# Operand addresses in SBUF: dense products of a two-block network, contiguous and at fixed offsets

## The chip, the cores and the metric

The kernel runs on one core of a Trainium2 chip. The metric is the device time of one execution in microseconds (us). Before the change the median of three runs is 1893.16 us (1890.84 to 1898.01).

## The reference, cut to what matters

The input is 256 tokens of width 1024, in float32. Two networks follow each other, each of two layers.

```python
# first network, layer i
h = rmsnorm(x, norm_mix_g[i])
mix = ...(h) @ w_out                     # layer 0: RWKV7 and gated delta rule; layer 1: banded attention
x = x + mix
x = x + square(relu(rmsnorm(x) @ mlp_w1[i])) @ mlp_w2[i]          # 1024 -> 4096 -> 1024
x = x + rmsnorm(p[i] @ ple_w_proj[i]) * sigmoid(x @ ple_w_gate[i])
# in layer 0's mixer a low-rank path reads the normed rows and the rows shifted by one token
dh = token_shift(h) - h
xw = h + dh * mu_lora[0]                 # likewise xa, xg;  then xw @ w1, xa @ a1, xg @ g1
# second network, layer i, on x and, in its layer 0, a second stream of 256 context tokens
x = x + gate * mixer(modulate(x)) @ w_out
x = x + gate * conv_ffn(modulate(x))     # up to 2 x 2816, a convolution over 3 tokens, silu * v, down
```

Nearly all the arithmetic is in the dense products with the weights `w_m` (MLP), `w_up` and `w_dn` (conv_ffn), and the projections of the mixers.

## The kernel before, in words

Activations lie feature-major: 128 features on the partitions, 256 tokens along a partition, and eight such slices make 1024 features. A dense product is made in float32r with both operands split in a high and a low part: `mm3` (line 433) issues high times high, low activation times high weight, high activation times low weight, each a matmul that loads 128 columns of weights and moves 256 columns of activations. Where two streams go together ("joint", `wide == 2`), one matmul moves 512 columns. `chunk` (line 442) goes over the output columns in pieces: a piece is 4 slices of 128 inputs by 256 outputs, so 24 matmuls. `weight` (line 420) issues a DMA of 512 KB from SP's queue into `raw` (4 buffers), and `split_w` lets ScalarE copy `raw` to `hi` and VectorE form `lo = raw - hi` (3 buffers each). `dense_tm` (line 1296) makes products token-major for attention: there the weights `hi`, `lo` are the moving operand, in runs of 256 columns, and the activations are loaded as weights.

The order of instructions on each engine is that of a scheduler, from priorities that the program sets; it interleaves small matmuls of the mixers (scores, transposes, recurrences) and of the norms with dense ones.

Where the operands lie, in bytes of a partition, in the built program:

- `act`, the tile of `acts` and `joint` (lines 529 and 534): rows of `T + 2` = 258 values, so 1032 bytes. `acts0` begins at 52800, `acts1` at 78272 (64 and 448 modulo 512), and each next slice lies 8 bytes further modulo 512 than the slice ahead of it.
- `hi` at 25792, 29888, 33984 and `lo` at 38080, 42176, 46272: all 192 modulo 1024, 4096 bytes long.
- `hh` and `hlo`, the 32 slices of the MLP's hidden activations (lines 1212 and 1213): rows of 256 values without a gap, at 107136 and 139904. Both are 128 modulo 512, and so is every slice.
- `fh` and `fl` in conv_ffn, as inputs of its first up-product (class `Early`, line 1740; 258 columns are used, two of them for a shift vector) and as hidden activations (`evac_v`, line 1840): rows of 1032 bytes, at many different offsets.

In `layer0_mixer` (line 992) the high and low parts `hh`, `hl_` are written from column 2 on, after GpSimd has set columns 0 and 1 to zero, so that `H` reads columns 2 to 257 and `HS`, the rows shifted by one token, columns 1 to 256 of the same tile. `lora` (line 1058) makes two products, `pa` from `H` and `pb` from `HS`, scales them with the row factors `rb` and `rbs` (the same factors, shifted) and adds them.

Of the kernel before, what the change touches and what calls it, by code (L numbers as in the profile page):

```python
# [10 lines left out]
F32 = mybir.dt.float32  # L11
# [8 lines left out]
P = 128  # L20
D = 1024
T = 256
KT = 8
NEG = -1.0e30
EPS = 1e-6
# [247 lines left out]
class K:  # L273
    def __init__(self, nc, tc, A, es):
        self.nc, self.tc, self.A, self.es = nc, tc, A, es
        self.cp = self.pool("const", 1)
        self.wraw = self.pool("wraw", 4)
        self.whi = self.pool("whi", 3)
        self.wlo = self.pool("wlo", 3)
        self.psG = self.pool("psG", 1, PSUM)  # L280
        self.sms = [self.pool(f"small{i}", 2) for i in range(3)]
        self.ap = [self.pool("acts0", 1), None]
        self.modp = self.pool("modp", 1)
        self.pse = None
        self.slots = None
        self.runs, self.head = False, None
        self.later, self.slow = [], []
# [131 lines left out]

    def weight(self, name, c, piece, kt, ncol, off=0):  # L420
        n = kt * ncol
        raw = self.wraw.tile([P, 1024], F32, name="raw")
        self.nc.sync.dma_start(out=raw[:, :n], in_=self.A[name][c, piece][:, off * ncol:off * ncol + n])
        return self.split_w(raw, n, kt)

    def split_w(self, raw, n, kt):
        hi = self.whi.tile([P, 1024], F32R, name="hi")
        lo = self.wlo.tile([P, 1024], F32R, name="lo")
        self.act(hi[:, :n], raw[:, :n])
        self.tt(lo[:, :n], raw[:, :n], hi[:, :n].bitcast(F32), ALU.subtract)  # L430
        return (hi[:, :n].rearrange("p (k n) -> p k n", k=kt), lo[:, :n].rearrange("p (k n) -> p k n", k=kt))

# [96 lines left out]
    def acts(self, i):  # L529

        t = self.ap[i].tile([P, 2, KT, T + 2], F32R, name="act", tag="act")
        return t[:, 0], t[:, 1]

    def joint(self):

        return [self.ap[i].tile([P, KT, 2, T + 2], F32R, name="act", tag="act") for i in range(2)]

# [74 lines left out]
def hl(h, l):  # L612
    return lambda j: (h[:, j], l[:, j])
# [378 lines left out]
def layer0_mixer(k, x, bg, ple):  # L992
# [20 lines left out]
    hh, hl_ = k.acts(0)  # L1013
    for t in (hh, hl_):
        nc.gpsimd.memset(t[:, :, 0:2].bitcast(F32), 0.0)
    st = k.stat_begin(None, "n0")
# [4 lines left out]
    for c in range(4):  # L1021
        xc = x[:, 2 * c:2 * c + 2]
        for e in range(2):
            j = 2 * c + e
            k.act(hh[:, j, 2:], xc[:, e], AF.Copy, scale=k.vec("gmix0", j))
            k.stt(hl_[:, j, 2:], xc[:, e], k.vec("gmix0", j), hh[:, j, 2:].bitcast(F32), ALU.mult, ALU.subtract)
    H = lambda j: (hh[:, j, 2:], hl_[:, j, 2:])
    HS = lambda j: (hh[:, j, 1:T + 1], hl_[:, j, 1:T + 1])
    rbp = big.tile([P, T + 2], F32, name="rbp")
    nc.gpsimd.memset(rbp[:, 0:2], 0.0)  # L1030
    rb, rbs = rbp[:, 2:], rbp[:, 1:T + 1]
    rb2 = rb[:, None, :].to_broadcast([P, 2, T])

    def norm():
        for c in range(4):
            k.stat_add(st, x[:, 2 * c:2 * c + 2], f2)
            yield
        k.norm_rows(st, rbp[:, 2:], lambda: f1("nt"))

# [18 lines left out]
    def lora():  # L1058

        pa, pb = (k.psD.tile([P, 2, T], F32, name="psx") for _ in range(2))  # L1060
        for half in range(2):
# [7 lines left out]
            k.tt(raw, raw, wb, ALU.subtract)  # L1069
            for src, X, ps in ((raw, H, pa), (wb, HS, pb)):  # L1070
                wh, wl = k.split_w(src, 1024, 4)
                for m in range(2):
                    ms = slice(m * P, (m + 1) * P)
                    for j in range(4):
                        k.mm3(ps[:, m], (wh[:, j, ms], wl[:, j, ms]), X(4 * half + j), half == 0 and j == 0 and m == 0, half == 1 and j == 3 and m == 1)
        z = w2.tile([P, 2, T], F32, name="dsh")
        k.tt(z, pb, rbs[:, None, :].to_broadcast([P, 2, T]), ALU.mult)
        k.tt(lt, pa, rb2, ALU.mult)
        k.tt(lt, lt, z, ALU.add)
        k.act(lt[0:64, 0], lt[0:64, 0], AF.Tanh)  # L1080
# [126 lines left out]
def mlp(k, l, x, xg, st, nxt, aside, aside2=None):  # L1207
# [3 lines left out]
    w2 = k.pool("mlpw", 2, es=es)  # L1211
    hh = hp.tile([P, 32, T], F32R, name="hh")
    hlo = hp.tile([P, 32, T], F32R, name="hlo")
# [83 lines left out]
def dense_tm(k, name, c, xs, evac):  # L1297

    ps = [k.psD.tile([P, 2, 256], F32, name="psx") for _ in xs]
    for pi in range(2):  # L1300
        wh, wl = k.weight(name, c, pi, 4, 256)
        for s, x in enumerate(xs):
# [437 lines left out]
class Early:  # L1740


    def __init__(self, k, mod, o, pool, n, s=0):
        self.k, self.mod, self.o, self.s = k, mod, o, s
        self.t = []
        for c in range(4):
            if 2 * c % n == 0:
                t = [pool.tile([P, n, T + 2], F32R, name=n_) for n_ in ("fh", "fl")]
            self.t.append([a[:, 2 * c % n:2 * c % n + 2] for a in t])
# [41 lines left out]
def conv_ffn(k, l, hs, hj, xs, mod, st0, sts, hp, early, between=None, out=None):  # L1791
# [36 lines left out]
    def evac_v(c, s, ps):  # L1828
# [10 lines left out]
        if c not in hid:  # L1839
            hid[c] = [hp.tile([P, 2 * ns, T + 2], F32R, name=n).rearrange("p (m s) t -> p m s t", m=2)[..., :T] for n in ("fh", "fl")]  # L1840
        k.split_act(hid[c][0][:, :, s], hid[c][1][:, :, s], o)
# [392 lines left out]
def program(nc, tc, A, out):  # L2234
    with ExitStack() as es:
        k = K(nc, tc, A, es)
        load_consts(k)
        k.mods = [k.modp.tile([P, 48, 2], F32, name=f"mod{l}") for l in range(2)]
        x = k.pool("xres", 1).tile([P, KT, T], F32, name="x")
# [54 lines left out]
```

## Time and profile before

| | |
|---|---|
| median of 3 runs | 1893.16 us (1890.84 to 1898.01) |
| profiled execution: its own time | 1898.16 us |
| profiled execution: span from first to last instruction | 1896.2 us |
| mean granted clock of TensorE | 0.985 |
| TensorE matmul / weight load busy | 1831.4 us / 1660.7 us |
| VectorE / ScalarE / GpSimd busy | 1383.3 us / 911.2 us / 75.4 us |
| moved by DMA | 292.13 MB, mean 154 GB/s |

Matmuls are pipelined: the profile's record of one lasts longer than the distance to the next one's start, so busy time and mean duration don't give the cost of a matmul in a full stream. What gives it is the distance from start to start, here called the **pace**: a stretch in which TensorE does nothing but one kind of matmul, divided by the number of matmuls in it. The windows view counts every instruction that touches the stretch; since a record is over two paces long, about two of those counted started ahead of it.

The groups of instructions are listed by line of the helper (`k.mm` is line 374 for every matmul), so a group is told by its tiles: `psx<-act,hi` is a matmul into the PSUM tile `psx` with `act` moving or loaded and `hi` as the other operand; the shape names the moving columns.

### The profile page before, as it was taken

The numbers are of one execution on the slowest core, as the hardware profiler recorded it, in microseconds if no ns is written. First come the engines' busy times: TensorE is split into PE (matmuls) and PEld (weight loads), VectorE is DVE, ScalarE is ACT, GpSimd is POOL, SyncE is SP. The second block draws the span as 40 slices with busy tenths as digits, with TensorE's granted clock in tenths as the row PEclk, the third lists the DMA queues.
The fourth block names the chain that finished last, engine by engine and source line by source line (L and its number), as shares of the span: only waits on it lengthen the run. The fifth ranks groups of instructions, "written<-read, shape, count | busy, mean of one in ns | idle before, by whom it ended". The sixth has DMA issues, their size and how long they took to land.

```text
span 1896.2 us, 36237 instructions
## 1 busy us (share of the span) xinstructions
PE 1831.4 (97%) x14540; PEld 1660.7 (88%) x14540; DVE 1383.3 (73%) x2874; ACT 911.2 (48%) x1526; POOL 75.4 (4%) x175
## 2 busy tenths in 40 slices
PE   7999999999999999999999897999999999899999
PEld 6777889999998899999988776878888998789998
DVE  6757668765687876768767888689785578977674
ACT  5433545554566755454545454433123444465443
POOL 0000010000000000000001100000000001100000
PEclk9999999999999999999999997999999999999999
DMA  8742414555563455654221122356872353334553
GB/s 314 269 163 106 139 57 130 187 189 191 190 212 127 158 194 188 195 190 163 84 65 49 36 72 86 100 210 196 275 252 89 123 185 127 100 101 151 184 189 123
DMA packets 80944, 292.13 MB, mean 154 GB/s; under 512 B 9255, under 2 KB 11144, under 8 KB 77448
## 3 DMA queue, kind: packets, MB, share of 16 engines
q1 hardware_dynamic: 80776, 289.82, 45.7%
q8 instruction: 114, 1.87, 0.4%
q14 instruction: 54, 0.44, 0.1%
HBM read 288.73 MB, written 1.05 MB: 153 GB/s over the span
## 4 chain that ended last, share of the span: by engine, by line
PE 86%; DVE 9%; ACT 2%; issue 1%; POOL 1%; DMA 1%; SPq 0%; ACTq 0%; DVEq 0%
PE psx L374 81%; DVE lo L364 3%; PE psx L377 2%; PE psg L1474 1%; PE psg L374 1%; ACT hi L361 1%; POOL qb L364 1%; DVE qx L364 0%; DVE mt L371 0%; DMA adaraw<-in_w_ada 0%; ACT act L361 0%; DVE act L371 0%; DVE act L364 0%; PE psg L377 0%; DVE qms L1329 0%
## 5 line engine op out<-in xcount | busy, mean ns | idle before, releaser
L374 PE MATMUL psx<-act,hi 128*128 128x256 f32 (+1 forms) x3872 | 821.0, 307 | 24.4 <-ACT hi L361 11.0
L361 ACT ACTIVATE hi<-raw 128x1024 fp32r<-128x1024 f32 (+1 forms) x440 | 453.8, 1032 | 631.9 <-PE psx L374 483.2
L364 DVE TENSOR_TENSOR lo<-raw,hi 128x1024 fp32r<-128x1024 f32 (+1 forms) x440 | 524.4, 1194 | 283.1 <-ACT hi L361 273.3
L374 PEld LDWEIGHTS psx<-act,hi 128*128 128x128 f32 x3872 | 630.4, 191 | 77.4 <-issue 14.4
L374 PE MATMUL psx<-act,lo 128*128 128x256 f32 (+1 forms) x1936 | 591.8, 306 | 4.8 <-DVE lo L364 4.8
L374 PEld LDWEIGHTS psx<-act,lo 128*128 128x128 f32 x1936 | 369.7, 191 | 29.0 <-DVE lo L364 7.3
L374 PE MATMUL psx<-hi,act 128*128 128x256 f32 x1280 | 242.1, 290 | 2.4 <-ACT act L361 1.5
L374 PEld LDWEIGHTS psx<-hi,act 128*128 128x128 f32 x1280 | 199.1, 191 | 10.4 <-issue 6.8
L374 PE MATMUL psx<-lo,act 128*128 128x256 f32 x640 | 181.0, 284 | 1.0 <-DVE lo L364 1.0
L374 PE MATMUL psx<-fh,hi 128*128 128x256 f32 (+2 forms) x528 | 162.3, 308 | 4.9 <-DVE xc L371 4.9
L374 PE MATMUL psx<-fh,lo 128*128 128x256 f32 (+2 forms) x528 | 162.3, 308 | 1.3 <-DVE lo L364 1.3
L374 PE MATMUL psx<-fl,hi 128*128 128x256 f32 (+2 forms) x528 | 161.7, 306 | 0.0
L374 PE MATMUL psx<-hh,hi 128*128 128x256 f32 x512 | 142.4, 278 | 0.0
L374 PE MATMUL psx<-hlo,hi 128*128 128x256 f32 x512 | 142.2, 278 | 0.0
L374 PE MATMUL psx<-hh,lo 128*128 128x256 f32 x512 | 142.2, 278 | 0.0
L374 PEld LDWEIGHTS psx<-lo,act 128*128 128x128 f32 x640 | 121.7, 191 | 1.2 <-DVE lo L364 1.2
L374 PEld LDWEIGHTS psx<-fh,hi 128*128 128x128 f32 x528 | 101.3, 192 | 10.9 <-issue 6.0
L374 PEld LDWEIGHTS psx<-fh,lo 128*128 128x128 f32 x528 | 101.2, 192 | 8.0 <-DVE lo L364 2.1
L374 PEld LDWEIGHTS psx<-fl,hi 128*128 128x128 f32 x528 | 101.3, 192 | 4.5
L374 PEld LDWEIGHTS psx<-hlo,hi 128*128 128x128 f32 x512 | 96.9, 189 | 0.0
L374 PEld LDWEIGHTS psx<-hh,hi 128*128 128x128 f32 x512 | 96.1, 188 | 0.0
L374 PEld LDWEIGHTS psx<-hh,lo 128*128 128x128 f32 x512 | 96.1, 188 | 0.0
(498 smaller groups left out, 2279.4 us busy)
## 6 DMA issues: line engine op xcount, KB each, us to landing
raw<-in_w_m SPq DMA_DIRECT2D x128, 512.0 KB, 4.3
raw<-in_w_up SPq DMA_DIRECT2D x92, 512.0 KB, 3.3
adaraw<-in_w_ada SPq DMA_DIRECT2D x24, 1024.0 KB, 6.2
adaraw<-in_w_ada SPq DMA_DIRECT2D x48, 512.0 KB, 4.3
raw<-in_w_dn SPq DMA_DIRECT2D x48, 512.0 KB, 3.4
raw<-in_w_ein SPq DMA_DIRECT2D x28, 512.0 KB, 5.5
raw<-in_w_ie SPq DMA_DIRECT2D x28, 512.0 KB, 3.3
raw<-in_w_qkv SPq DMA_DIRECT2D x24, 512.0 KB, 3.3
```

The costliest lines, as they stand in the source:

```text
L361: self.nc.scalar.activation(out=out, in_=in_, func=func, **kw)
L364: (eng or self.nc.vector).tensor_tensor(out=out, in0=a, in1=b, op=op)
L374: self.pe(lambda: self.nc.tensor.matmul(out=out, lhsT=lhsT, rhs=rhs, start=start, stop=stop))
L377: self.pe(lambda: self.nc.tensor.transpose(out=out, in_=in_, identity=self.ident))
L1474: k.pe(lambda: nc.tensor.matmul(out=ps[q:q + 32], lhsT=sv[:, 4 * pi + j], rhs=raw[:, j], start=pi == 0, stop=pi == 1, tile_position=(0, q)))
```

## The change

Every operand of a dense product becomes a contiguous run at one offset. `acts` and `joint` lose the two columns (rows of 1024 bytes), and a joint operand of 512 columns is one run. The two `mod` tiles move ahead of `acts0` and get padding of 40 values each, so that `acts0` lies at 60032 and `acts1` at 84608, both 128 modulo 512. The weight tiles become 1280 values long, so at 25792, 30912, 36032 and 41152, 46272, 51392: again 192 modulo 1024. `dense_tm` uses them from value 96 on: its moving weights lie at 64 modulo 512, the activations that it loads at 128. `fh` and `fl` get lead-in padding that puts them at 128 modulo 512 (in `Early` the second row of a pair, still 258 values long, is 8 bytes further). `hh` gets 112 values of lead-in; `hh` and `hlo` stay at 128 modulo 512.

In `layer0_mixer` there is no shifted operand: `pb` is made from `H` too, scaled with `rb`, and added to `pa` with a shift by one column (255 of 256 columns). Two memsets of `act` and one of `rbp` on GpSimd are gone.

On TensorE, VectorE, ScalarE and SP's queue the same instructions stand in the same order as before (TensorE 9119 rows in both, VectorE 2365, ScalarE 1059, SP 210). What is different is their addresses, some shapes (two runs of 256 become one of 512, the last addition of `lora` 2 x 255 in place of 512), and waits: three waits of TensorE on DMAs of the context tiles, issued long before, come in where a pool now overlaps another. GpSimd has three memsets fewer.

```diff
-    def weight(self, name, c, piece, kt, ncol, off=0):
+    def weight(self, name, c, piece, kt, ncol, off=0, pad=0):
...
-    def split_w(self, raw, n, kt):
-        hi = self.whi.tile([P, 1024], F32R, name="hi")
-        lo = self.wlo.tile([P, 1024], F32R, name="lo")
-        self.act(hi[:, :n], raw[:, :n])
-        self.tt(lo[:, :n], raw[:, :n], hi[:, :n].bitcast(F32), ALU.subtract)
...
+        return self.split_w(raw, n, kt, pad)
+
+    def split_w(self, raw, n, kt, pad=0):
+
+        hi, lo = (p.tile([P, WLEN], F32R, name=nm)[:, pad:pad + n] for p, nm in ((self.whi, "hi"), (self.wlo, "lo")))
+        self.act(hi, raw[:, :n])
+        self.tt(lo, raw[:, :n], hi.bitcast(F32), ALU.subtract)
...
     def acts(self, i):
 
-        t = self.ap[i].tile([P, 2, KT, T + 2], F32R, name="act", tag="act")
+        t = self.ap[i].tile([P, 2, KT, T], F32R, name="act", tag="act")
...
-        return [self.ap[i].tile([P, KT, 2, T + 2], F32R, name="act", tag="act") for i in range(2)]
+        return [self.ap[i].tile([P, KT, 2, T], F32R, name="act", tag="act") for i in range(2)]
...
     hh, hl_ = k.acts(0)
-    for t in (hh, hl_):
-        nc.gpsimd.memset(t[:, :, 0:2].bitcast(F32), 0.0)
...
-    H = lambda j: (hh[:, j, 2:], hl_[:, j, 2:])
-    HS = lambda j: (hh[:, j, 1:T + 1], hl_[:, j, 1:T + 1])
-    rbp = big.tile([P, T + 2], F32, name="rbp")
-    nc.gpsimd.memset(rbp[:, 0:2], 0.0)
-    rb, rbs = rbp[:, 2:], rbp[:, 1:T + 1]
+    H = hl(hh, hl_)
+    rb = big.tile([P, T], F32, name="rbp")
...
-            for src, X, ps in ((raw, H, pa), (wb, HS, pb)):
+            for src, X, ps in ((raw, H, pa), (wb, H, pb)):
...
-        k.tt(z, pb, rbs[:, None, :].to_broadcast([P, 2, T]), ALU.mult)
+        k.tt(z, pb, rb2, ALU.mult)
         k.tt(lt, pa, rb2, ALU.mult)
-        k.tt(lt, lt, z, ALU.add)
+        k.tt(lt[:, :, 1:], lt[:, :, 1:], z[:, :, :T - 1], ALU.add)
...
-    hh = hp.tile([P, 32, T], F32R, name="hh")
+    hh = hp.tile([P, HPAD + 32 * T], F32R, name="hh")[:, HPAD:].rearrange("p (k t) -> p k t", k=32)
...
-        wh, wl = k.weight(name, c, pi, 4, 256)
+        wh, wl = k.weight(name, c, pi, 4, 256, pad=WPAD)
...
-                t = [pool.tile([P, n, T + 2], F32R, name=n_) for n_ in ("fh", "fl")]
+                t = [pool.tile([P, n * T + 128], F32R, name=n_)[:, FPAD:FPAD + n * (T + 2)].rearrange("p (n t) -> p n t", n=n) for n_ in ("fh", "fl")]
...
-            hid[c] = [hp.tile([P, 2 * ns, T + 2], F32R, name=n).rearrange("p (m s) t -> p m s t", m=2)[..., :T] for n in ("fh", "fl")]
+            hid[c] = [hp.tile([P, 2 * ns * T + 128], F32R, name=n)[:, FPAD:FPAD + 2 * ns * T].rearrange("p (m s t) -> p m s t", m=2, s=ns) for n in ("fh", "fl")]
```

with `MPAD = 40`, `WPAD = 96`, `WLEN = 1024 + 256`, `FPAD = 104`, `HPAD = 112`.

## Rows read from the trace of the kernel before

**Rows 1.** the page: span and busy time of each engine

```profile
span 1896.2 us, 36237 instructions
PE 1831.4 (97%) x14540; PEld 1660.7 (88%) x14540; DVE 1383.3 (73%) x2874; ACT 911.2 (48%) x1526; POOL 75.4 (4%) x175
```

**Rows 2.** the page: the chain that ended last, shares of the span by engine

```profile
PE 86%; DVE 9%; ACT 2%; issue 1%; POOL 1%; DMA 1%; SPq 0%; ACTq 0%; DVEq 0%
```

**Rows 3.** TensorE groups by shape: xcount | busy us, mean ns | idle us

```profile
L374 PE MATMUL psx<-act,hi 128*128 128x256 f32 x3200 | 607.2, 288 | 23.2 <-ACT hi L361 11.0 <-ACT act L361 7.4 <-DVE xc L371 1.8
L374 PE MATMUL psx<-hi,act 128*128 128x256 f32 x1280 | 242.1, 290 | 2.4 <-ACT act L361 1.5 <-DVE act L371 0.9
L374 PE MATMUL psx<-fh,hi 128*128 128x256 f32 x336 | 94.7, 282 | 0.0
L374 PE MATMUL psx<-fh,hi 128*128 128x258 f32 x96 | 29.7, 313 | 4.9 <-DVE xc L371 4.9
L374 PE MATMUL psx<-act,hi 128*128 128x512 f32 x672 | 213.8, 399 | 1.2 <-DVE fl L364 1.0 <-ACT fh L361 0.2
L374 PE MATMUL psx<-fh,hi 128*128 128x512 f32 x96 | 37.9, 395 | 0.0
L374 PE MATMUL psx<-hh,hi 128*128 128x256 f32 x512 | 142.4, 278 | 0.0
```

**Rows 4.** six stretches: start:end length, TensorE busy (instructions), clock, DMA share, rate

```profile
415.00:490.00 75.00, 75.00 (x664) 1.00 0.59 194
746.00:770.00 24.00, 24.00 (x214) 1.00 0.57 190
775.00:830.00 55.00, 55.00 (x470) 1.00 0.59 191
670.00:740.00 70.00, 70.00 (x591) 1.00 0.56 184
1815.00:1870.00 55.00, 54.99 (x465) 1.00 0.52 173
1430.00:1480.00 50.00, 50.00 (x217) 1.00 0.27 90
```

**Rows 5.** operand hh, second MLP: ns min/median/max, first to last start us

```profile
L374 PE MATMUL psx<-hh,hi x256: 276/281/468, 744.5 to 834.0; 128*128 128x256 f32 x128
```

**Rows 6.** TensorE in order of time at 771.4 us: start us, us, what

```profile
771.60 0.28 PE L374 MATMUL psx<-hh,lo 128*128 128x256 f32 x1
771.72 0.59 PE L374 MATMUL psx<-sacc,ct 128*128 128x256 f32 x2
771.96 0.47 PE L374 MATMUL psx<-hh,hi 128*128 128x256 f32 x1
772.26 0.28 PE L374 MATMUL psx<-hlo,hi 128*128 128x256 f32 x1
```

**Rows 7.** pieces of the chain, the four longest: start us, us, what

```profile
306.05 232.97 PE psx L374 x1984
654.36 204.59 PE psx L374 x1725
1237.05 306.86 PE psx L374 x1516
1711.72 157.51 PE psx L374 x1309
```

**Rows 8.** ScalarE and VectorE groups in 415 to 490 us

```profile
L361 ACT ACTIVATE hi<-raw 128x1024 fp32r<-128x1024 f32 x28 | 29.8, 1063 | 42.4 <-PE psx L374 41.3 <-issue 1.1
L364 DVE TENSOR_TENSOR lo<-raw,hi 128x1024 fp32r<-128x1024 f32 x28 | 34.3, 1225 | 33.3 <-ACT hi L361 33.3
```

**Rows 9.** 1311 to 1411 us: PE, PEld, DVE, ACT, POOL busy, clock, DMA

```profile
1311.00:1411.00 100.00, 100.00 (x429) 80.87 (x429) 79.02 (x126) 23.27 (x27) 0.36 (x4) 1.00 0.77 257
```

**Rows 10.** a TensorE group in 1815 to 1870 us

```profile
L374 PE MATMUL psx<-fh,lo 128*128 128x256 f32 x24 | 6.8, 285 | 0.0
```

**Rows 11.** a GpSimd memset in 0 to 30 us

```profile
L1015 POOL MEMSET act<- 128x16 f32 x2 | 0.2, 114 | 0.3 <-POOLq L2287 0.3
```

More of the change, by code (lines that the diff above doesn't have):

```diff
@@ L23 @@
 KT = 8
+MPAD = 40
+WPAD = 96
+WLEN = 1024 + 256
+FPAD = 104
+HPAD = 112
 NEG = -1.0e30
@@ L281, in __init__ @@
         self.sms = [self.pool(f"small{i}", 2) for i in range(3)]
+        self.modp = self.pool("modp", 1)
+        self.mods = [self.modp.tile([P, 96 + MPAD], F32, name=f"mod{l}")[:, :96].rearrange("p (j s) -> p j s", s=2) for l in range(2)]
         self.ap = [self.pool("acts0", 1), None]
-        self.modp = self.pool("modp", 1)
         self.pse = None
@@ L423, in weight @@
         self.nc.sync.dma_start(out=raw[:, :n], in_=self.A[name][c, piece][:, off * ncol:off * ncol + n])
-        return self.split_w(raw, n, kt)
-    def split_w(self, raw, n, kt):
-        hi = self.whi.tile([P, 1024], F32R, name="hi")
-        lo = self.wlo.tile([P, 1024], F32R, name="lo")
-        self.act(hi[:, :n], raw[:, :n])
-        self.tt(lo[:, :n], raw[:, :n], hi[:, :n].bitcast(F32), ALU.subtract)
-        return (hi[:, :n].rearrange("p (k n) -> p k n", k=kt), lo[:, :n].rearrange("p (k n) -> p k n", k=kt))
+        return self.split_w(raw, n, kt, pad)
[3 more added lines that the diff above has]
+        self.tt(lo, raw[:, :n], hi.bitcast(F32), ALU.subtract)
+        return (hi.rearrange("p (k n) -> p k n", k=kt), lo.rearrange("p (k n) -> p k n", k=kt))
     def mm3(self, ps, w, x, first, last):
@@ L1024, in layer0_mixer @@
             j = 2 * c + e
-            k.act(hh[:, j, 2:], xc[:, e], AF.Copy, scale=k.vec("gmix0", j))
-            k.stt(hl_[:, j, 2:], xc[:, e], k.vec("gmix0", j), hh[:, j, 2:].bitcast(F32), ALU.mult, ALU.subtract)
-    H = lambda j: (hh[:, j, 2:], hl_[:, j, 2:])
-    HS = lambda j: (hh[:, j, 1:T + 1], hl_[:, j, 1:T + 1])
-    rbp = big.tile([P, T + 2], F32, name="rbp")
-    nc.gpsimd.memset(rbp[:, 0:2], 0.0)
-    rb, rbs = rbp[:, 2:], rbp[:, 1:T + 1]
+            k.act(hh[:, j], xc[:, e], AF.Copy, scale=k.vec("gmix0", j))
+            k.stt(hl_[:, j], xc[:, e], k.vec("gmix0", j), hh[:, j].bitcast(F32), ALU.mult, ALU.subtract)
+    H = hl(hh, hl_)
+    rb = big.tile([P, T], F32, name="rbp")
     rb2 = rb[:, None, :].to_broadcast([P, 2, T])
@@ L1037, in norm @@
             yield
-        k.norm_rows(st, rbp[:, 2:], lambda: f1("nt"))
+        k.norm_rows(st, rb, lambda: f1("nt"))
     rst = big.tile([P, T], F32, name="rst")
@@ L2237, in program @@
         load_consts(k)
-        k.mods = [k.modp.tile([P, 48, 2], F32, name=f"mod{l}") for l in range(2)]
         x = k.pool("xres", 1).tile([P, KT, T], F32, name="x")
```

## The prediction, made before the result was known

> **What bounds the kernel now.** I read the page first, then the chain of waits, then TensorE's groups by shape, and last the windows of stretches in which TensorE does one thing. The page: a span of 1896.2 us with a matmul record open 97% of it [rows 1]. The chain that ended last runs over TensorE for 86% of the span and over VectorE for 9% [rows 2], and four of its pieces are nothing but dense matmuls [rows 7]: 232.97 + 204.59 + 306.86 + 157.51 = 901.9 us in which no other engine and no DMA comes in. So TensorE is the bound, and what matters is how fast one dense matmul follows another: the pace.
>
> The pace is read from the windows [rows 4], with two taken off each count for the matmuls that began ahead of the window.
>
> - `hh`, `hlo`, first MLP (operands at 128 modulo 512, without gaps): 75 us / 662 = **113.3 ns**; second MLP, 746 to 770 us: 24 / 212 = 113.2 ns.
> - `hh`, `hlo`, second MLP, 775 to 830 us: 55 / 468 = **117.5 ns**.
> - `act` in rows of 1032 bytes: 70 / 589 = 118.8 ns, and 55 / 463 = 118.8 ns in a window of the last conv_ffn, where `fh` and `fl` take part. Joint, 512 columns: 50 / 215 = 232.6 ns.
>
> The granted clock is 1.00 in all six rows, the full one of its two levels (2.4 GHz), and the DMA share is no higher where the pace is slow (0.27 to 0.59), so neither makes the difference. What differs between the first and the fourth row is where the operands lie. But lying well is not all: in the second MLP the same tiles at the same addresses go from 113.2 to 117.5 ns in mid-stream. What stands there is one matmul of the norms (`sacc,ct`), after which the stream starts anew at 771.96 us [rows 6]. So an aligned stream has at least **two paces**, and what interrupts it can change which one it is in. The duration column shows this too: the minimum of `psx<-hh,hi` is 276 ns, the median of the second MLP 281 [rows 5].
>
> **The change part by part.**
>
> *Matmuls of 256 columns that are not aligned now.* `act,hi` 3200 and half as many `act,lo`, 1600; `hi,act` 1280 and half as many `lo,act`, 640; three `fh`/`fl` groups of 336; three of 96 with 258 columns (which I count here) [rows 3]: 8016. All get the addresses that `hh` and `hi` have: 128 against 192 modulo 512, or in the token-major products 64 against 128, the same distance. The trace of before has no run of `act` at these addresses, so I bound the pace by `hh`: 113.3 below, 117.5 above (that it could be slower than now is a rival). Which to take? `hh` runs 768 matmuls of the first MLP at the fast pace, and of the second, from 744.5 [rows 5] to 771.6 us, 27.1 / 0.1133 = 239; so 1007 of 1536, 66%. I take that mix: 0.66 x 113.3 + 0.34 x 117.5 = 114.7 ns. Gain: 8016 x (118.8 - 114.7) = 32.9 us. Ends: 44.1 us (all fast), 10.4 us (all slow).
>
> *Matmuls of 512 columns.* `act` 672 + 336, `fh`/`fl` three times 96 [rows 3]: 1296 at 232.6 ns. Two paces of 256: 2 x 114.7 = 229.4. Gain 1296 x 3.2 = 4.1 us. Ends: 226.6 ns gives 7.8 us; 235 ns, above today's, loses 3.1 us.
>
> *`hh` itself* keeps its addresses; which pace it falls in is drawn anew. With the same mix nothing; ends +2.2 us (529 matmuls by 4.2) and -4.2 us (1007).
>
> *The first mixer* has as many matmuls and VectorE operations as before; two memsets of 114 ns [rows 11] and a like one go, on an engine that works 4% of the span [rows 1]: 0. The added waits on old context DMAs and the wider layout: 0, since those tiles were read hundreds of us before.
>
> *What hides the rest.* A piece of 24 matmuls needs 1063 ns of ScalarE and 1225 ns of VectorE for its weights [rows 8], against 24 x 113.3 = 2719 ns of TensorE; the first MLP's down product already runs at that pace with both waiting. In 1311 to 1411 us VectorE is at 79.0% and DMA at 0.77 of the stretch [rows 9]; 2.6% faster makes 81% and 0.79. The cover holds. It doesn't in the mixers, where dense matmuls fill in between chains of small work. There TensorE holds the chain for 0.86 x 1896 - 902 = 729 of 994 us, 73%; I let 73% of a gain there reach the end. Dense work in all: 8016 x 118.8 + 1296 x 232.6 + 1536 x 114.7 ns = 1430 us, of it 902 in the long pieces; of what is not `hh` (176 us, all in the pieces) 726 us count in full and 528 at 73%, mean 0.887.
>
> **Sum:** 37.0 x 0.887 = 33 us. The profiled execution took 1898.2 us, 5 above the median (0.3%, within the runs' spread); the windows are shares of a span that long, and I take the gain from the median: 1893 - 33 = **1860 us**.
>
> **A rule against it.** Rows 4 and 6 say that the pace depends on where both operands lie and on how the stream starts, as if the loading of weights and the moving of columns met somewhere. The Trainium skill, "TensorE: Matmul & The Clock Gate", section "Step-by-step: what each phase is for", says that TensorE has two independent read ports of SBUF, one for the moving operand and one for the weights, so that loading the next weights takes nothing from the running matmul. By that, the offset between the two would not matter, and this change would be worth nothing: 1893 us. The trace does not agree in full: 113.3 and 118.8 ns at one clock need some cause, and contiguous rows at one offset are all that sets the two streams apart. It is a rival below.
>
> **The rivals.**
>
> 1. *Fast pace throughout.* The regular streams keep 113.3 ns: 44.1 + 7.8 + 2.2 = 54.1, x 0.887 = 48 us, **1845 us**. For it: both `hh` streams began fast, without a break from the product ahead. Against: [rows 6]. Chance 0.20.
> 2. *Slow pace nearly throughout.* Every stream that starts after a small matmul locks at 117.5 ns as at 771.96 us; and since aligned streams follow each other, `hh` inherits it. 10.4 - 3.1 - 4.2 = 3 us at worst, 10 us without the last two: 1884 to 1890, about **1888 us**. For it: the one restart that the trace shows. Chance 0.16.
> 3. *The change doesn't do what it says.* The pace comes from something else in the MLP's down product (32 slices in a row, one output tile for 192 matmuls) and not from addresses. Then nothing: **1893 us**. Against: the up product's matmuls are alike in all but the address. Chance 0.08.
> 4. *Slower.* With mixed offsets each matmul meets a different phase, good and bad average out at 118.8 ns. With one offset everywhere a stream can lock in a bad phase and stay. A bad phase as the trace shows it: `fh,lo` in the last conv_ffn, 285 ns per record against 281 at 117.5 [rows 10, 5], so some 122 ns. 8016 x 3.2 x 0.887 = 23 us: **1916 us**. It decides from a mean pace of 120.1 ns on (1.3 ns x 8016 x 0.887 = 9.5 us, 0.5%). Against: neither of the two paces seen is above today's mean. Chance 0.06.
>
> **How the numbers follow.** The mix has a chance of 0.50; every result in it, from 1850 to 1880 us, is faster by over 0.5% (below 1884 us), which is about what a measurement of this kernel can tell from no change. Fast throughout adds 0.20, and of the slow case about 0.04 lies below 1884. Faster: 0.74. Same: 0.12 + 0.08 = 0.20. Slower: 0.06. The range leaves out the changed-nothing and slower cases and the edge of the fast one: 1842 to 1890 us.
>
> **What would show it.** The windows of the changed kernel: the pace of `act` in the four long pieces, at 113.3 or at 117.5 ns; changes from one to the other in mid-stream, right behind a `sacc,ct` or another small matmul; medians of 276 or 281 ns in the records. Fewer chain pieces by VectorE would say that the mixers gained less than 73%. Wrong would be: a pace of `act` of 118.8 as before (rival 3), one above 120 (rival 4), or dense matmuls at the fast pace while the end doesn't move, which would mean that I misread who holds the chain.

## The result, and the profile after

The changed kernel takes 1877.8 us (median of 6 runs, 1873.3 to 1881.4), the kernel before in the same comparison 1896.2 us (6 runs, 1890.8 to 1902.8): a ratio of **0.9897**, with a 95% interval of 0.9875 to 0.9919. It is faster by more than 0.5%, and inside the range; but of the 33 us that I forecast some 18 came.

Two times come up below that are no medians: the profiled execution of before has a span of 1896.2 us, that of the changed kernel 1876.0, 20.2 us less. The page of the changed kernel:

```profile
span 1876.0 us, 36239 instructions
PE 1806.1 (96%) x14540; PEld 1633.4 (87%) x14540; DVE 1381.0 (74%) x2874; ACT 911.0 (49%) x1526; POOL 75.2 (4%) x172
```

The same number of matmuls, and 25 us less in which one is open; VectorE and ScalarE work as long as before [rows 1]. (The page's chain of waits follows only the last 1% of this execution, so I read nothing from it.) TensorE's groups by shape, the counterparts of [rows 3]:

```profile
L380 PE MATMUL psx<-act,hi 128*128 128x256 f32 x3200 | 588.8, 285 | 23.7 <-ACT hi L367 11.8 <-ACT act L367 7.1 <-DVE xc L377 2.0
L380 PE MATMUL psx<-hi,act 128*128 128x256 f32 x1280 | 238.2, 288 | 2.6 <-ACT act L367 1.7 <-DVE act L377 0.9
L380 PE MATMUL psx<-act,hi 128*128 128x512 f32 x672 | 214.1, 400 | 1.3 <-DVE fl L370 1.2
L380 PE MATMUL psx<-hh,hi 128*128 128x256 f32 x512 | 141.9, 277 | 0.0
L380 PE MATMUL psx<-fh,hi 128*128 128x258 f32 x96 | 30.4, 320 | 4.9 <-DVE xc L377 4.9
```

256 columns got shorter (288 to 285, 290 to 288 ns), 512 did not (399 to 400), 258 got longer (313 to 320). The windows show the pace, again with two taken off each count (columns as in [rows 4]):

```profile
415.00:490.00 75.00, 75.00 (x664) 1.00 0.60 192
680.00:750.00 70.00, 70.00 (x596) 1.00 0.59 187
775.00:830.00 55.00, 55.00 (x488) 1.00 0.63 203
1420.00:1470.00 50.00, 50.00 (x216) 1.00 0.27 90
1715.00:1840.00 125.00, 125.00 (x1105) 1.00 0.61 196
```

The first MLP runs at 75 / 662 = 113.3 ns and the last conv_ffn at 125 / 1103 = 113.3 ns; the up product of the second MLP runs at 70 / 594 = 117.8 ns, its down product at 55 / 486 = 113.2 ns; the joint products stand at 50 / 214 = 233.6 ns. So the two paces that the prediction read from `hh` come up again in the other aligned streams; in these windows of 256 columns nothing lies between them.

Where does one become the other? The timeline of the changed kernel at 765 us (columns as in [rows 6]):

```profile
765.44 0.28 PE L380 MATMUL psx<-hh,lo 128*128 128x256 f32 x1
765.56 0.60 PE L380 MATMUL psx<-sacc,ct 128*128 128x256 f32 x2
765.81 0.47 PE L380 MATMUL psx<-hh,hi 128*128 128x256 f32 x1
766.11 0.28 PE L380 MATMUL psx<-hlo,hi 128*128 128x256 f32 x1
```

It is the matmul of the norms (`sacc,ct`) that stands at 771.72 us in [rows 6]. There the stream went from 113.2 to 117.5 ns behind it, here from 117.8 to 113.2. So behind the same small matmul a stream can take either pace.

TensorE's matmuls stand in the same order in both kernels, so the start of the same matmul in both traces cuts the two spans into the same stretches. What my sum gave each stretch follows from its own prices: 4.1 ns for each matmul of 256 or 258 columns that was not `hh`, 3.2 ns for one of 512, times 0.73 outside the long pieces:

```
stretch (time in before)      before   changed   gain   my sum
start to first MLP, 0-306      306.1     303.4    2.7    2.6
first MLP, 306-539             233.0     228.2    4.8    4.9
mixer, 539-654                 115.3     115.4   -0.1    2.0
second MLP, 654-859            204.6     202.3    2.3    3.9
mixers, 859-1237               378.3     378.5   -0.2    5.3
joint products, 1237-1544      306.6     305.3    1.3    5.2
mixer, 1544-1712               168.1     165.9    2.2    2.5
last conv_ffn, 1712 to end     184.1     177.0    7.1    6.1
```

Three quarters of what is missing in this execution are in two rows: the mixers from 859 to 1237 us, and the joint products. The row ahead of the first MLP agrees, but that can be luck: in the last experiment below the same stretch gained 3.8 us with the paces of before.

### The profile page after: what moved, and what is told of

Read it like the earlier page. It is cut to its first block, busy times and chain, and to the rows that moved or that the text cites. A ratio compares the mean times of both kernels' runs of the same rounds, so it can differ in the third digit from the quotient of the medians.

```text
span 1876.0 us, 36239 instructions
## 1 busy us (share of the span) xinstructions
PE 1806.1 (96%) x14540; PEld 1633.4 (87%) x14540; DVE 1381.0 (74%) x2874; ACT 911.0 (49%) x1526; POOL 75.2 (4%) x172
## 5 line engine op out<-in xcount | busy, mean ns | idle before, releaser
L380 PE MATMUL psx<-act,hi 128*128 128x256 f32 (+1 forms) x3872 | 802.9, 305 | 25.1 <-ACT hi L367 11.8
L367 ACT ACTIVATE hi<-raw 128x1024 fp32r<-128x1024 f32 (+1 forms) x440 | 454.0, 1032 | 599.1 <-PE psx L380 452.6
L380 PEld LDWEIGHTS psx<-act,hi 128*128 128x128 f32 x3872 | 623.2, 190 | 78.6 <-ACT hi L367 15.2
L380 PE MATMUL psx<-hi,act 128*128 128x256 f32 x1280 | 238.2, 288 | 2.6 <-ACT act L367 1.7
L1505 DVE CUSTOM_DVE_ANT_0 adat<-adaraw,adac 128x1024 f32<-128x1024 f32 x64 | 78.3, 1223 | 25.0 <-DMA adaraw<-in_w_ada 23.1
```

The source lines that it names most:

```text
L367: self.nc.scalar.activation(out=out, in_=in_, func=func, **kw)
L380: self.pe(lambda: self.nc.tensor.matmul(out=out, lhsT=lhsT, rhs=rhs, start=start, stop=stop))
L1505: nc.vector.tensor_tensor_reduce(out=t, in0=raw, in1=row[:, s], scale=1.0, scalar=0.0, op0=ALU.mult, op1=ALU.add, accum_out=mod[:, j, s:s ...
```

## The experiments

Below, **distance** is the offset of the moving run minus that of the operand which is loaded for the same matmul, modulo 256 bytes. In the changed kernel it is 128 - 192 = 192 (modulo 256) for the feature-major products, which load weights, and 64 - 128 = 192 for the token-major ones, which load activations. The streams alone are programs with one execution each. Means of a pace are taken from start to start of dense matmuls that follow each other in the program; intervals over 1.2 times the pace are left out, since something else ended those.

**Which offset is worth what.** A stream of matmuls alone, with nothing else at work, at each offset of the moving run in steps of 32 bytes; weights at 192 modulo 512, operands without gaps. The edit is a program of its own around the kernel's `mm` and `split_w`:

```diff
+        for off in range(0, 512, 32):
+            stream(f"s256r{r}o{off}x", off, 4, 256, 256)
```

> This kernel computes nothing of the reference: its output is a copy of part of the input. It loads weights at 192 modulo 512, as the changed kernel does, and runs streams of 96 matmuls of 256 columns (in the same order of high and low parts) with all moving runs at one offset modulo 512, one stream for each multiple of 32, twice, each started behind one float32 matmul; then six more starts at offset 128, three streams at 132, 136 and 144, and four at rows of 1032, 1040, 1056 and 1088 bytes. No other engine works meanwhile. Theory A (the offset between moving run and loaded weights sets which paces there are, and the start picks one): at 128 only 113.3 and 117.5 ns occur, and some other offsets show other paces, 116.6 ns at 480 as in the products of ple; the rows of 1032 bytes give 118.8. Theory B (contiguous runs on whole lines are all that matters): every multiple of 16 shows the same two paces, and only 132, 136 and the rows of 1032 bytes are slower.

Windows of the second round, moving run at 0, 64, 128 and 192:

```profile
202.00:212.00 10.00, 10.00 (x87) 1.00 0.01 2
226.00:236.00 10.00, 10.00 (x86) 1.00 0.00 0
249.50:259.50 10.00, 10.00 (x90) 1.00 0.01 2
273.00:283.00 10.00, 10.00 (x86) 1.00 0.01 2
```

From start to start it is 117.78, 120.00, **113.33** and 120.00 ns; 32 to 224 in the odd steps give 117.8 to 120.0, and 256 to 480 repeat 0 to 224 to 0.05 ns. All ten streams at 128 modulo 256 hold 113.33 ns; 4, 8 or 16 bytes beside it, the pace is 119 to 122. Runs in rows of 1032, 1040, 1056 and 1088 bytes, the first of them at 128, take 120.4, 117.8, 118.8 and 118.3 ns. No traffic of another engine is needed for any of it, at a granted clock of 1.00, the full level.

**The same for 512 columns.**

```diff
+            stream(f"w512r{r}o{off}x", off, 3, 512, 512)
```

> This kernel, too, computes nothing of the reference; its output is a copy of part of the input. It is the same scan with matmuls of 512 columns, contiguous, 72 in a stream. In the changed kernel these take 233.3 ns at 128, where I had counted on 229.4. Theory A: there are offsets with another pace, down to twice 113.3 = 226.7 ns, and 128 is not one of them. Theory B: all offsets give 233 ns, since a contiguous run of 512 columns costs that.

Windows of the second round at 0, 128 and 192:

```profile
289.00:304.00 15.00, 15.00 (x67) 1.00 0.00 1
357.00:372.00 15.00, 15.00 (x66) 1.00 0.00 0
392.00:407.00 15.00, 15.00 (x68) 1.00 0.00 0
```

228.9, 233.3 and **226.67** ns from start to start; every other offset 233.3 or 234.3. So 512 columns want offset 192, which is distance 0, where 256 columns are at their worst. At offset 128 (distance 192), where the change puts them, they run at 233.3: not faster than the 232.96 of the kernel before.

**Without gaps, but at another offset.** The changed kernel with the padding ahead of `acts0` taken out, so that all activation operands of dense products lie at 320 modulo 512. That is distance 128 for the feature-major products; the token-major ones, with moving weights at 64, get distance 0:

```diff
-MPAD = 40
+MPAD = 0
```

> The changed kernel with the padding of the two small tiles ahead of the activations taken away, so that every contiguous activation operand (act, fh, fl, hh, hlo) lies at 320 modulo 512 in place of 128; the weights stay at 192. Theory A: other paces than 113.3 and 117.5 ns, of the order of the 116.6 ns that another offset showed, so some 8000 matmuls at 1.3 ns more than the 115.3 ns of the changed kernel: 10 us slower, 1888 us. Theory B: no difference, 1878 us within 4.

1903.1 us, **1.0031** of the kernel before (1.0017 to 1.0046), with a window of its first MLP that reads

```profile
415.00:490.00 75.00, 75.00 (x635) 1.00 0.55 184
```

or 118.5 ns. That is 25 us above the changed kernel, where I had expected 10. Contiguous rows as such are worth nothing here; `hh` too falls back to 118.7 ns, and takes some 6 us with it (1536 x 3.8 ns). The gain hangs on the offset.

**Token-major weights where they were.** Distance 64 instead of 192 in `dense_tm`, the rest as changed:

```diff
-WPAD = 96
+WPAD = 0
```

> The changed kernel with the weights of the token-major products back at 192 modulo 512 (moving), while the activations that are loaded there stay at 128: the distance between the two is turned around, 64 bytes below in place of 64 above. Theory A: those 1920 matmuls get other paces, by up to 3 ns, so 2 to 6 us slower than the changed kernel's 1878 us, and the groups hi,act and lo,act show longer records than 288 and 282 ns. Theory B: no difference.

1878.0 us, 0.9891 (0.9874 to 0.9908): no difference to the changed kernel that can be measured, though the token-major pace goes from 115.0 to 117.3 ns. That is 1920 x 2.3 = 4.4 us of TensorE's time, of which the prediction's 73% would be 3.2 us. With intervals of about 3 us to either side, and a mean granted clock of 0.988 in these four executions against 0.983 in the first six of the changed kernel, such an effect is neither shown nor excluded.

**The changed kernel once more**, for the paces of its streams.

> The changed kernel again, unaltered. Theory A1 (which of the two paces an aligned stream holds is set by how its start falls against the instructions ahead of it, and that repeats from run to run): the up product of the second MLP again holds 117.8 ns a matmul from about 656 to 765 us, and the first MLP again 113.3 ns from 328 to 510 us. Theory A2 (the start falls by chance): some of the long stretches hold the other pace this time. The time is 0.989 of the kernel before by both, within 0.002.

1877.5 us, 0.9884 (0.9867 to 0.9901). Windows of this execution:

```profile
415.00:490.00 75.00, 75.00 (x664) 1.00 0.57 193
680.00:750.00 70.00, 70.00 (x620) 1.00 0.60 195
775.00:830.00 55.00, 55.00 (x469) 1.00 0.55 192
```

The first MLP runs as in the first execution; the second MLP the other way round, up at 113.3 and down at 117.8 ns. The code and its addresses are the same, so the pace that a start takes changes from run to run.

**Starts by themselves.** Streams at 128 behind different small matmuls, twice over.

```diff
+                stream(f"d{kind}{n}r{r}x", 128, 2, 256, 256, (kind, n))
```

> Computes nothing of the reference (its output is a copy of part of an input): streams of matmuls alone, all other engines idle. 38 starts of 48 matmuls each, with the moving run at 128 modulo 256 and 256 columns, behind one to eight transposes, one to eight 64-column products, or one to three 256-column products; then 258-column streams at 0, 64, 128 and 192, and two runs of 256 columns taken as one operand of 512 at 128 and at 192. Theory A1 (the start alone decides which of the two paces an aligned stream holds): about a quarter of the 38 hold 117.8 ns and the others 113.3. Theory A3 (the slower pace needs the traffic of the other engines): all 38 hold 113.3. The 258-column streams: 120 to 122 ns at every offset, slower than 256 columns by more than their 2 columns. The split 512 at 192: 226.7, as the contiguous one, if the length of a row is all that matters; 228 to 234 if the gap of 2 values costs.

The rows of four streams by tile (ns min/median/max, first to last start): behind two transposes, eight transposes, two 64-column products, one 256-column float32 product. As in [rows 5], a median of 276 is the pace of 113.3 ns, 281 that of 117.8.

```profile
L380 PE MATMUL dt2r0x<-arena,hi x32: 276/276/365, 19.4 to 24.7; 128*128 128x256 f32 x32
L380 PE MATMUL dt8r0x<-arena,hi x32: 281/281/363, 55.8 to 61.3; 128*128 128x256 f32 x32
L380 PE MATMUL ds2r0x<-arena,hi x32: 281/281/384, 68.1 to 73.6; 128*128 128x256 f32 x32
L380 PE MATMUL dm1r0x<-arena,hi x32: 276/276/469, 113.9 to 119.3; 128*128 128x256 f32 x32
```

18 of the 38 hold the slower pace with no other engine at work: both streams behind eight transposes and all 16 behind the short products; 19 hold the faster one, and the first of all, which ran partly at the lower clock, tells nothing. So other engines' traffic isn't needed. Within this program the same start gave the same pace twice, wherever both can be compared. Streams of 258 columns: 119.0 to 120.8 ns at any offset. Of the two runs taken as one operand at 192, those in rows of 258 values give 233.1 ns, the contiguous ones 226.7: the gap of two values costs all that the offset gives.

**Address or distance.** Four places of the weights, four of the run, three starts each (`s` two short products, `m` one float32 product, `t` eight transposes).

```diff
+    for w in (0, 64, 128, 192):
+        W = weights(w)
+        for off in (0, 64, 128, 192):
+            for kind, n in (("s", 2), ("m", 1), ("t", 8)):
+                stream(f"w{w}o{off}{kind}x", off, 2, 256, 256, (kind, n), W)
```

> Computes nothing of the reference (its output is a copy of part of an input): streams of 48 matmuls of 256 columns alone, all other engines idle. Weights at 0, 64, 128 and 192 modulo 256, moving run at 0, 64, 128 and 192, each pair behind three starts: two 64-column products (which gave 117.8 ns at weights 192, run 128), one 256-column float32 product (113.3 there), eight transposes (117.8 there). Theory A4 (only the place of the moving run counts, the pace is its reading): runs at 128 give 113.3 or 117.8 by their start with any weights, all others 117.8 to 120. Theory A5 (the distance between weights and run counts): the best pairs lie on a diagonal, run 192 above the weights modulo 256: weights 0 with run 192, 64 with 0, 128 with 64, 192 with 128; 113.3 there, 117.8 to 120 elsewhere. Open in both: whether a pair gives 113.3 behind all three starts; a kernel with such a pair would have no second pace to fall into.

Rows by tile; the numbers in a name are the offset of the weights and of the run:

```profile
L380 PE MATMUL w0o64sx<-arena,hi x32: 276/276/384, 34.0 to 39.3; 128*128 128x256 f32 x32
L380 PE MATMUL w0o64mx<-arena,hi x32: 279/279/467, 39.8 to 45.4; 128*128 128x256 f32 x32
L380 PE MATMUL w0o192mx<-arena,hi x32: 280/281/469, 77.7 to 83.3; 128*128 128x256 f32 x32
L380 PE MATMUL w0o192tx<-arena,hi x32: 276/276/367, 84.3 to 89.6; 128*128 128x256 f32 x32
L380 PE MATMUL w64o0mx<-arena,hi x32: 276/276/469, 96.1 to 101.6; 128*128 128x256 f32 x32
L380 PE MATMUL w64o64mx<-arena,hi x32: 280/283/467, 114.9 to 120.6; 128*128 128x256 f32 x32
L380 PE MATMUL w192o128mx<-arena,hi x32: 276/276/470, 284.1 to 289.5; 128*128 128x256 f32 x32
L380 PE MATMUL w192o192mx<-arena,hi x32: 281/283/468, 302.8 to 308.5; 128*128 128x256 f32 x32
```

The distance counts. At distance 0 all twelve streams run at 120.0 ns (one row here: 283), at 128 all at 118.5 to 120.0. At 192, whatever the weights' place, 7 of 12 hold 113.3 and 5 hold 117.8 ns. What I had not expected: distance 64 has the same two paces, 4 of 12 at 113.3, and these four are the ones behind two short products. No pair takes the faster pace behind all three starts. And `w192o128s` holds 113.3 ns, where the same start in the program above held 117.8: the kind of the matmul ahead doesn't settle it either.

**Both moved in the kernel.** The kernel of MPAD 0, with the weights moved after the runs: distance 192 again, and no operand of a 256-column product at the place modulo 256 that it had in the changed kernel.

```diff
-MPAD = 40
+MPAD = 0
...
-        hi, lo = (p.tile([P, WLEN], F32R, name=nm)[:, pad:pad + n] for p, nm in ((self.whi, "hi"), (self.wlo, "lo")))
+        hi, lo = (p.tile([P, WLEN], F32R, name=nm)[:, pad + 48:pad + 48 + n] for p, nm in ((self.whi, "hi"), (self.wlo, "lo")))
```

> The kernel that had every moving operand of the dense products at 64 bytes modulo 256 (MPAD 0, 1.0031 of the kernel before), with one thing more: all weight tiles 192 bytes further on, so that weights lie at 128 modulo 256 (token-major ones at 0). Each run is again 192 above its weights modulo 256, as in the changed kernel, but no operand of a 256-column product lies where it lay there. Theory A5 (the distance between run and weights sets the pace): all of the gain comes back, 0.989 of the kernel before, within 0.003; the 256-column means 114.5 to 116 ns. Theory A4 (the place of the run by itself): 1.003 as without the move; means 118.7 to 119.5.

1873.9 us, **0.9872** (0.9854 to 0.9890): all of the gain is back, 1.6% below the same kernel with the weights unmoved. The means are 114.9 and 115.5 ns. With the experiment at distance 128 it shows the cause in the kernel itself, since the two differ in the place of the weights alone.

**The joint operands at distance 0.** 1248 of the 1296 matmuls of 512 columns:

```diff
+JPAD = 16
...
-            hid[c] = [hp.tile([P, 2 * ns * T + 128], F32R, name=n)[:, FPAD:FPAD + 2 * ns * T].rearrange("p (m s t) -> p m s t", m=2, s=ns) for n in ("fh", "fl")]
+            f = FPAD + (JPAD if ns == 2 and c < 6 else 0)
+            hid[c] = [hp.tile([P, 2 * ns * T + 128], F32R, name=n)[:, f:f + 2 * ns * T].rearrange("p (m s t) -> p m s t", m=2, s=ns) for n in ("fh", "fl")]
...
-    hj = k.joint()
+    hj = k.joint(JPAD)
```

> The changed kernel with the joint operands (the two streams side by side, 512 columns) and the operands of the joint down products moved from 128 to 192 bytes modulo 256; their weights stay at 0. That is 1248 of the 1296 512-column matmuls. Theory A (the offset of the moving run sets the pace of the matmul stream, and 512 columns want 192): their mean falls from 233.3 to 226.7 ns; in the stretches where TensorE streams without a stop that is 1248 x 6.6 ns = 8.2 us, less what other engines take back, so 5 to 8 us below the changed kernel (a ratio to it of 0.9957 to 0.9973), and 25 to 28 us below the kernel before. Theory B (these stretches are held by VectorE and the weight transfers, not by TensorE): the matmuls get shorter but the time stays within 2 us of the changed kernel.

(The weights lie at 192 modulo 256, not at 0 as that text says; moving the run to 192 is what makes the distance 0.) 1871.7 us, **0.9857** (0.9835 to 0.9878), 5.8 us below the second set of executions of the changed kernel: the lowest median of all, though the two intervals overlap. Its windows:

```profile
415.00:490.00 75.00, 75.00 (x640) 1.00 0.54 187
1420.00:1470.00 50.00, 50.00 (x222) 1.00 0.29 98
```

The joint products run at 50 / 220 = 227.3 ns, and the stretch from 1237 to 1544 us takes 298.6 us against 305.3 in both profiled executions of the changed kernel: 6.7 us, so TensorE does bound it. The first MLP of this execution took the slower pace (75 / 638 = 117.6 ns).

**Distance 64 in the kernel**, with the joint operands kept at 0:

```diff
-        hi, lo = (p.tile([P, WLEN], F32R, name=nm)[:, pad:pad + n] for p, nm in ((self.whi, "hi"), (self.wlo, "lo")))
+        hi, lo = (p.tile([P, WLEN], F32R, name=nm)[:, pad + 32:pad + 32 + n] for p, nm in ((self.whi, "hi"), (self.wlo, "lo")))
...
-JPAD = 16
+JPAD = 48
...
-            f = FPAD + (JPAD if ns == 2 and c < 6 else 0)
+            f = FPAD + (JPAD - 64 if ns == 2 and c < 6 else 0)
```

> The kernel with the joint operands at 192 (0.986 of the kernel before), with all weight tiles 128 bytes further on and the joint operands moved along with them to 64: the 256-column runs stay at 128 and are now 64 above their weights modulo 256 (192 before), the 512-column runs are at distance 0 as before. Theory A5 with both odd distances alike (streams alone held 113.3 or 117.8 ns at 64 and at 192): 0.986 of the kernel before, within 0.004 (which of the two paces each long stream takes is open, some 5 us either way); 512-column mean 227. If the pace of 512 columns went by the run's place alone (A4): 233.3 and 6 to 8 us more, about 0.990. If starts at distance 64 lock to 113.3 less often than at 192 (behind a float32 product 0 of 4 did there, 2 of 4 at 192), the 256-column means go from 115 towards 117.8 and the time to 0.990 as well, with the 512-column mean at 227.

1886.2 us, **0.9940** (0.9926 to 0.9953). The last case named: the joint products keep their pace, the others lose theirs.

```profile
415.00:490.00 75.00, 75.00 (x639) 1.00 0.54 187
775.00:830.00 55.00, 55.00 (x470) 1.00 0.57 196
1420.00:1470.00 50.00, 50.00 (x223) 1.00 0.29 101
```

117.7, 117.5 and 226.2 ns. Of the kernel's 123 starts of 256-column streams of ten matmuls or more that hold one of the two paces, 11 hold 113.3 ns; at distance 192 it is 88 of 119, 85 of 123, 81 of 123 and 78 of 122 in four executions (changed, changed again, joint at 0, both moved). So distances 64 and 192 both allow both paces, and 192 gets the good one about seven times in ten.

A small matmul in between isn't needed for a change of pace. In the changed kernel the feature-major products behind the first MLP hand over to token-major ones at 513.14 us without a break, from weights that are loaded to weights that move. Windows ahead of that point and behind it:

```profile
500.00:513.00 13.00, 13.00 (x117) 1.00 0.60 203
513.20:517.20 4.00, 4.00 (x36) 1.00 0.56 178
```

From start to start the pace goes from 113.3 to 117.8 ns there. Each execution has three long handovers of this sort, two from feature-major to token-major and one back. In the four executions at distance 192 all twelve swap the pace, seven from 113.3 to 117.8 and five the other way. With distance 64 on both sides (this kernel) or on the token-major side alone (`WPAD = 0`) all six come in at 117.8 and stay there.

**The first mixer alone.** The kernel before, its low-rank products taking the plain operand and the shift made on their result:

```diff
-            for src, X, ps in ((raw, H, pa), (wb, HS, pb)):
+            for src, X, ps in ((raw, H, pa), (wb, H, pb)):
...
-        k.tt(lt, lt, z, ALU.add)
+        k.tt(lt[:, :, 1:], lt[:, :, 1:], z[:, :, :T - 1], ALU.add)
```

> The kernel before with one part of the change alone: the first mixer's low-rank products take the plain operand, and the shift by one token is made on their result; all addresses of the dense products stay. My sum has nothing for this part: within 3 us of the kernel before (ratio 0.9985 to 1.0015). The rival, that the removed shift (operands and scale at odd offsets) was worth something by itself: 4 us or more.

1895.4 us, 0.9982 (0.9972 to 0.9992): 3.3 us less, just past my bound, and the paces are those of before (118.9 and 118.5 ns). In the profiles, the same matmul starts 0.8 us later than in before at 220 us, long after the part that was changed, and 3.8 us earlier at 260. The time parts there. TensorE's windows in before:

```profile
228.00:232.00 4.00, 4.00 (x20) 0.50 0.21 84
232.00:236.00 4.00, 4.00 (x20) 0.50 0.02 4
```

and in this kernel:

```profile
228.00:232.00 4.00, 4.00 (x27) 0.72 0.35 126
232.00:236.00 4.00, 4.00 (x32) 0.86 0.01 4
```

A matmul was open all the time in both windows, and the granted clock lies at 0.50, the lower level, for less long here. Other executions with this part differ there again (the changed kernel: 0.54 and 0.60). That is where this execution gained. The ten executions of this kernel have a mean granted clock of 0.986, the 17 of before in the same comparison 0.985, so a little more of the full level goes with the gain in the others too; whether the part brings it about, or only the draw of the clock, these runs don't tell. Up to 3 of the 18 us of the whole change may thus have nothing to do with operands of the dense products. The difference between distance 128 and both moved doesn't contain it, since both kernels have this part.

All kernels side by side, mean pace in ns by kind of product (`fm` feature-major, `tm` token-major, 258 columns of `Early`, 512 columns of the joint products), and the ratio to the kernel before:

```
                     256 fm   256 tm     258      512      hh     to before
before               118.92   118.61   120.41   232.96   114.89
changed              114.68   115.00   121.39   233.31   114.04   0.9897
changed, again       114.46   115.09   121.09   233.32   114.86   0.9884
distance 128         118.72   119.54   119.80   233.21   118.67   1.0031
tm at 64             115.00   117.26   121.33   233.32   117.09   0.9891
both moved, 192      114.93   115.51   121.31   233.35   117.08   0.9872
joint at 0           115.35   114.73   121.39   227.09   117.08   0.9857
joint at 0, 64       117.56   117.55   119.36   226.97   117.78   0.9940
first mixer alone    118.93   118.52   120.32   232.96   114.89   0.9982
```

## Why the prediction was right, and where it was not

**Right: the bound and the mechanism.** TensorE's pace sets the time of the long pieces, and it goes by where the operands lie. I forecast 114.7 ns for 256 columns, a mix of 113.3 and 117.5; it is 114.7 feature-major and 115.0 token-major, a mix of 113.3 and 117.8. In the last conv_ffn the gain came about as worked out (7.1 against 6.1 us; 6.7 to 7.3 in the four other executions whose feature-major products are at distance 192), where it holds 113.3 ns each time. In the first MLP 4.8 against 4.9 us is a lucky draw: so it was again in the second execution, but with `WPAD = 0`, both moved and joint at 0 that stretch fell into 117.8 ns and took 1.5 to 2.0 us longer than before. `hh` drew its pace anew, as said: 114.0, 114.9, 117.1 and 117.1 ns in the four executions that leave it at 128 modulo 512 and at distance 192, and 117.1 with both moved. What I called an aligned stream, though, is one at a distance of 192: the run without gaps and at one offset was what the prediction saw, and at distance 128 such runs took 1.0031 of the time before.

**Wrong: matmuls of 512 columns** (4.1 us). I took twice the pace of 256. They have a best distance of their own: 226.7 ns at 0, 233.3 at the 192 that the change gives them. It came out at 0.3 ns x 1296 = 0.5 us lost, inside the ends of that term (7.8 gained, 3.1 lost), at its bad one. The good end was to be had 64 bytes further on.

**Wrong: 258 columns counted as 256.** 288 matmuls, 1.0 ns slower instead of 4.1 faster: 1.5 us.

TensorE's time fell by 5808 x 4.24 + 1920 x 3.61 + 1536 x 0.85 ns, less these, or 32 us where I had 37. At 0.887, my share of a gain that reaches the end, that is 4.4 us of the 14 us missed.

**Wrong: the share that reaches the end, in part for the clock.** I took the share of the chain that TensorE holds in the mixers, 73%, for the share of a gain there that reaches the end, and had no term for TensorE's clock. At the end of the first profiled execution stand 20.2 of 32 us, 0.63 and not 0.887: 8 us, the larger part of the miss. But that execution is the odd one. The same quotient, the gain of the span by the gain in TensorE's time from the table of paces, is 0.77 in the second execution of the same kernel (24.6 of 32.0 us), and 0.80, 0.81 and 0.79 for `WPAD = 0`, both moved and joint at 0. What the traces show to set the first one apart is the clock: by their records TensorE stood at the lower level for 67.3 us in it, against 58.0 in before and 50.0 to 56.9 in the four others. Nine microseconds more at half the full clock are worth up to 4.7 us (an estimate, as if TensorE were the bound all that time).

The mixers between 859 and 1237 us show it. These are windows from the same matmul to the same matmul in before, changed, changed again and both moved (busy us and count of PE, PEld, DVE, ACT, POOL; clock, DMA, rate):

```profile
858.97:1237.32 378.35, 354.44 (x2592) 313.54 (x2590) 289.52 (x798) 193.42 (x437) 24.72 (x36) 0.96 0.25 81
849.28:1227.75 378.47, 354.43 (x2592) 313.84 (x2591) 289.83 (x798) 193.19 (x437) 24.77 (x36) 0.95 0.25 81
844.68:1221.07 376.39, 350.98 (x2592) 309.53 (x2590) 289.77 (x798) 193.27 (x438) 24.75 (x36) 0.96 0.24 81
853.76:1227.64 373.88, 348.41 (x2592) 307.18 (x2591) 289.62 (x798) 193.14 (x438) 24.76 (x36) 0.97 0.24 82
```

My sum had 5.3 us for this stretch, 7.25 in full. It gained nothing in the first execution, 2.0 us in the second and 4.5 with both moved; at the lower clock it spent 41.0, 30.7 and 23.9 us, and 30.7 in before. TensorE's idle time, the length less the busy time, is 23.9 us in before and 24.0, 25.4 and 25.5 in the others, so at most 1.6 us of the gain went into waits. Such waits there are: from 1100 to 1140 us, in before already, VectorE is busy 91% of the time.

```profile
1100.00:1140.00 40.00, 33.69 (x239) 29.80 (x237) 36.22 (x118) 23.88 (x61) 0.15 (x2) 0.99 0.24 78
```

So in the executions that spent no more time at the lower clock than before, some four fifths of TensorE's gain reached the end where I had 0.887. Whether 73% is right for the mixers by themselves, these runs don't tell: the clock moves the stretch by as much as the change does. Nor do they tell whether faster matmuls lower the clock: eleven executions of the changed kernel have a mean granted clock of 0.980 to 0.987.

**A slip.** In the fourth rival 1.3 ns x 8016 x 0.887 is 9.2 us, not 9.5; nothing hangs on it.

**The rivals.** Slow nearly throughout (1888 us) is what distance 64 does: 11 of 123 starts at the faster pace, and 0.9940 even with the joint products at their best. Fast throughout didn't come up, since starts draw their pace. The lock in a bad phase (slower) needs another distance: 120.0 ns at 0, 118.5 to 120.0 at 128. That the change does nothing (1893 us) is refuted: one distance between the loaded operand and the run gives 120.0 ns, another 113.3, with nothing else at work. The Trainium skill, "TensorE: Matmul & The Clock Gate", section "Step-by-step: what each phase is for", says that TensorE has two independent read ports, so that loading the next weights takes nothing from the running matmul. These streams don't agree with what I drew from it, that the offset between the two would not matter. Where the loading and the run would meet the runs don't tell.

**Left open:** why the distance matters, what sets which pace a start takes, why handovers swap it, and whether a pace can be forced. If all long streams held 113.3 ns, the profiled execution of the joint version would have some 3900 x 4.4 ns = 17 us less of TensorE's time (an estimate; 3900 matmuls stand in its streams of ten or more at 117.8). A start forced to the faster pace wasn't tried.

## What to carry to other kernels

Where matmuls stream one behind the other with a weight load each, read the pace from windows, from start to start, and look where run and weights lie relative to each other: a scan of offsets with a stream alone costs one run and tells the best distance for each length of run, which need not be the same for 256 and 512 columns. Put several kinds of small matmuls ahead of the streams: behind the one kind of the first scan each distance showed a single pace. Price such a gain stretch by stretch, in full only where TensorE alone is busy. And a pace that depends on how a stream starts, and a clock that differs between executions, make one profile a single draw: before explaining why a stretch gained nothing, cut a second execution at the same matmuls, and compare the granted clock as well as the idle time.

## What the runs showed of the hardware that I had not expected

- The pace of 256 float32r columns with a weight load each depends on the distance between run and loaded operand with a period of 256 bytes: 120.0 ns at 0, 118.5 to 120.0 at 128, 113.3 or 117.8 at 64 and at 192. At 2.4 GHz, 113.33 ns are 272 cycles for 256 columns, 120.0 are 288.
- 512 columns are best where 256 are worst: 226.67 ns at distance 0, 233.3 at 192.
- A run in two pieces with a gap of 8 bytes (233.1 ns) loses what the offset gives (226.7).
- With the same code and addresses, a stream of some hundred matmuls holds 113.3 ns in one execution and 117.8 in the next. At distance 192 it changes behind small matmuls and, without any interruption, where feature-major products hand over to token-major ones or back: all twelve long handovers of four executions swapped the pace.
